# Four reorderings in the mixer of a one-layer hybrid decoder step: state update, decay heads 2 and 3, the copy out of the transposes, and the rank of the convolution's window copies

## The chip, the cores and the metric

The kernel runs on one core of a Trainium2 chip. The metric is the device time of one execution in microseconds (us), as the median of the runs shown. TensorE appears in the profile as PE (matmuls) and PEld (weight loads), VectorE as DVE, ScalarE as ACT, GpSimd as POOL, and the queue of the sync engine, which starts most DMA transfers, as SP.

## What is computed

One layer of a decoder, applied to a prompt of 16 + 256 tokens and to 8 running sequences of 8 new tokens each, 336 token columns in all. The layer projects the normalised input once and feeds two branches, a Conformer convolution and a Mamba-2 mixer, joins them, and then runs a mixture over 16,384 single-row experts (PEER). The change lies in the two branches:

```
c = causal_depthwise(conf_cat, conf_dw_w, conf_dw_b)          # 31 taps, 1024 channels
xbc_c = silu(causal_depthwise(m_cat, m_conv_w, m_conv_b))      # 4 taps, 4096 channels
...
acs   = cumsum(dt * A)                                         # per head
decay = exp(where(causal, acs[t] - acs[s], -inf))
y     = einsum((C B^T) * decay, dt * x) + einsum(C, h) * exp(acs)
h_new = exp(last) * h + einsum(B, w_end * dt * x)              # state update
```

The 32 heads form 8 groups of 4. After the mixer come the two output projections, the join, and the experts: for 128 tokens the chosen expert rows are gathered from HBM, and for the other tokens all experts are computed densely from streamed blocks.

## The kernel before, in words

**Layout.** Channels lie on the 128 partitions and tokens on the free axis. Each of the 80 blocks of 128 output channels of the input projection is one `project()` call: 24 matmuls of 336 (or 320) columns into one PSUM tile of the tag `pj`, which has three buffers. The weights are split in two parts, `wh` (ACT, L243) and `wl` (mostly POOL, L247), with two buffers each, so that a projection multiplies high by high, high by low and low by high.

**The groups.** A loop over the 8 head groups overlaps two things: the projections of the next group and the state-space work of the present one. `ssd(g, ...)` (L617) is a generator whose steps are separated by `yield`; after each projection the loop advances it by one step (`run(new, 1)`), and its last steps run among the next group's projections (`run(old, 1)`). In one group the projections are, in this order: the convolution's value and gate blocks (`conf`, L583), four blocks of x, B and C (`xbc`, L556), and two blocks of the output gate z (`zproj`, L574). The steps of `ssd`, numbered from 0:

- 0: spread the sample tokens of x and B; `decay(0)`, `decay(1)`
- 1: `turn(0)` (three transposes of chunk 0), `decay(2)`
- 2: `turn(1)`, `turn(2)`, `decay(3)`, copies of C
- 3: `running()` (the states of the 8 sequences), `inner(0)`
- 4 and 5: `inner(1)`, `state(0)`; `inner(2)`, `state(1)`
- 6: `state(2)`, `out(0)`
- 7: `out(1)`
- 8: squares of the output, `update()` (eight matmuls and four adds into the states `st`), the DMA of `st` to HBM
- 9: the norm's sum over channels (`pgn`)

**What sets the order.** The PE instructions of the mixer keep the order of the program text. On the other engines a scheduler orders the instructions at build time by priority and by its own estimate of when each is ready; every engine then executes its list strictly in order, and a wait at the head of a list holds up all behind it. `tc.cur_priority` is the rank that the scheduler uses; instructions made while it is raised by `LOW` (400) come later where there is a choice. `act()` (L219) also keeps its activations in program order, and an `ACT_TABLE_LOAD` stands in front of an activation when its function is not in the table that is loaded; exponential and sigmoid or SiLU need different tables.

**PSUM tiles that the steps share.** `pj` has three buffers: every projection takes one and, in `xbc`, keeps it until the SiLU of the short convolution has been read from it, because the convolution's taps are accumulated in the same tile (`conv_short`, L522). `misc` has two buffers (transposes, `pcb`, `pst`, `pq`). `y` has two (`pdec`, `py`, `po`). `update()` takes two `misc` and two `pj` tiles. `pb` has one, for the long convolution.

**The long convolution.** `conv_long` (L504) first copies the 31-column windows of its input into the tile `ch` (`windows`, L494: ACT copies at L499 and L501), then does the first tap on ACT (L517) and the other 30 on DVE (L519), all at low rank. Its result for the last channel block is needed by `norm_mean` (L817) in the last group, in front of the normalisation and of the output projection `conf_out` (L807).

Of the kernel before, what the change touches and what calls it, by code (L numbers as in the profile page):

```python
# [60 lines left out]
LOW = 400  # L61
# [97 lines left out]
def body(tc, ia, oa, stop=None):  # L159
    nc = tc.nc  # L160
    with ExitStack() as top:
# [189 lines left out]
        p = misc([128, T], "pn1")  # L351
# [137 lines left out]
        def samp(ap):  # L489
            return ap.rearrange("p (q c) -> p q c", q=NQ)  # L490
# [3 lines left out]
        def windows(cat):  # L494
            win = mp.tile([128, KD * T2], F32, name="ch")[:, :NCH * WIN]
            wv = win.rearrange("p (c i) -> p c i", i=WIN)
            a_ = cat[:, NM:NM + 1]
            np_ = SQ // TS
            nc.scalar.copy(wv[:, :np_], bass.AP(tensor=a_.tensor, offset=a_.offset,  # L499
                                                ap=[list(a_.ap[0]), [TS, np_], [1, WIN]]))  # L500
            nc.scalar.copy(wv[:, np_:], samp(cat[:, CC + TP:]))  # L501
            return wv

        def conv_long(cat, j, dst):  # L504
            wv = windows(cat)
            acc = ps.tile([128, T], F32, name="pcv", tag="pb", bufs=1)[:, :T2]
            at = tc.cur_priority
            tc.cur_priority = at + LOW

            def eights(v):  # L510
                return v.rearrange("p (c i) -> p c i", i=TS)

            for w in range(CW):
                sc = V("conf_w", j * CW + w)
                in_, to = wv[:, :, w:w + TS], eights(dst if w == CW - 1 else acc)
                if w == 0:
                    nc.scalar.activation(to, in_, AF.Identity, scale=sc, bias=V("conf_b", j))  # L517
                else:
                    nc.vector.scalar_tensor_tensor(to, in_, sc, eights(acc), op0=OP.mult, op1=OP.add)  # L519
            tc.cur_priority = at  # L520
# [96 lines left out]
        def ssd(g, xg, bc, sz):  # L617
# [8 lines left out]
            def decay(r):  # L626
                h = 4 * g + r
                pb = ps.tile([128, T], F32, name="pdec", tag="y", bufs=2)[:, :T2]
                mm(pb, id3[:, h:h + 1].to_broadcast([128, 128]), acs3[:, :T2], start=True, stop=True)
                hs_ = slice(r % 2 * 64, r % 2 * 64 + 64)  # L630
                act(e2[hs_, r // 2], pb[hs_], AF.Exp)
                for i, (t0, L) in enumerate(OTILES):
                    nc.vector.scalar_tensor_tensor(dec[:, r, t0:t0 + L], pb[:, t0:t0 + L], acs[i][:, h:h + 1],
                                                   mneg[:, t0:t0 + L], op0=OP.add, op1=OP.add)
                if r % 2:
                    act(dec[:, r - 1:r + 1], dec[:, r - 1:r + 1], AF.Exp)
# [4 lines left out]
            def turn(i):  # L641
                p = misc([128, 384], "ptr")
                for c_, src in enumerate((xg[:, 0], xg[:, 1], BT)):
                    tr(p[:, c_ * 128:(c_ + 1) * 128], chunk(src, i, c_), ident)
                x_ = sp.tile([128, 384], F32, name=f"xt{i}")
                nc.scalar.copy(x_[:, 256:], p[:, 256:])
                nc.vector.tensor_tensor(r4(x_[:, :256]), r4(p[:, :256]),
                                        dtok[i][:, 4 * g:4 * g + 4, None].to_broadcast([128, 4, P]), op=OP.mult)
                w_ = sp.tile([128, 4, P], F32, name=f"wx{i}")
                nc.gpsimd.tensor_tensor(w_, r4(x_[:, :256]),  # L650
                                        wd[i][:, 4 * g:4 * g + 4, None].to_broadcast([128, 4, P]), op=OP.mult)
                xt.append(x_)
                wx.append(w_.rearrange("p r c -> p (r c)"))
# [29 lines left out]
            def out(b):  # L683
                py = ps.tile([128, T], F32, name="py", tag="y", bufs=2)[:, :T2]
                po = ps.tile([128, T], F32, name="po", tag="y", bufs=2)[:, :T2]
                bs = slice(b * 128, b * 128 + 128)
                for i, (t0, L) in enumerate(OTILES):
                    for r in (2 * b, 2 * b + 1):
                        s = slice((r % 2) * 64, (r % 2) * 64 + 64)
                        mm(py[s, t0:t0 + L], xt[i][:, r * P:(r + 1) * P], dec[:, r, t0:t0 + L],  # L690
                                         start=True, stop=True)
                mm(po[:, SQ:], oq[:, bs], C("selq")[:, :S0], start=True, stop=True)
                for i in (1, 2):
                    t0, L = TILES[i]
                    mm(po[:, t0:t0 + L], hs[i - 1][:, bs], CT[:, t0:t0 + L], start=True, stop=True)
                y = xg[:, b, :T2]
                nc.vector.scalar_tensor_tensor(y, y, V("dskip", 2 * g + b), py, op0=OP.mult, op1=OP.add)
                yo = tp.tile([128, T], F32, name="yo", bufs=2)[:, :T2]
                nc.vector.tensor_tensor(yo, po, e2[:, b], op=OP.mult)
                nc.gpsimd.tensor_tensor(y, y, yo, op=OP.add)  # L700
                nc.gpsimd.tensor_tensor(y, y, sz[:, b, :], op=OP.mult)

            def update():
                four = [f() for _ in range(2) for f in (
                    lambda: misc([128, 512], "pst2"), lambda: ps.tile([128, PJ], F32, name="pst2", tag="pj", bufs=3))]
                for r in range(2):
                    for s_ in range(4):
                        t_ = slice(32 * s_, 32 * s_ + 32)
                        mm(four[s_][:, r * 256:(r + 1) * 256], Bm[t_, r], wx[0][t_], start=True, stop=True)
                for s_ in (1, 3, 0, 2):  # L710
                    sv = st[:, 2 * s_:2 * s_ + 2].rearrange("p q c -> p (q c)")
                    nc.vector.tensor_tensor(sv, sv, four[s_], op=OP.add)  # L712
# [5 lines left out]
            yield  # L718
            turn(0)
            decay(2)  # L720
            yield
            turn(1)
            turn(2)
            decay(3)
            for s_ in range(2):
                nc.scalar.copy(cz[:, 4 * s_:4 * s_ + 4, 8 * s_:8 * s_ + 8],
                               CT[:, SQ + 32 * s_:SQ + 32 * s_ + 32].rearrange("p (q t) -> p q t", q=4))
# [15 lines left out]
            out(0)  # L743
            yield
            out(1)
            yield
            sq = [tp.tile([128, T2], F32, name="sq", bufs=4) for _ in range(2)]
            for b in range(2):
                nc.scalar.activation(sq[b], xg[:, b, :T2], AF.Square)
            nc.gpsimd.tensor_tensor(sq[0], sq[0], sq[1], op=OP.add)  # L750
            update()
            nc.sync.dma_start(oa["ssm_s"][g], st)
            yield
            p = pj2("pgn")
# [178 lines left out]
        for j in range(KD):  # L933
# [4 lines left out]
            p = pj2()  # L938
# [7 lines left out]
        for j in range(KD):  # L946
            w = weight(ia["w_o"], j)
            p = pj2()
# [13 lines left out]
        p = ps.tile([128, T], F32, name="pn2", tag="pb", bufs=1)  # L962
# [38 lines left out]
        for c_ in range(2):  # L1001
            p = misc([128, 512], "px")
# [4 lines left out]
        p = misc([128, 4], "prs")  # L1007
# [178 lines left out]
        for j in range(16):  # L1186
# [5 lines left out]
            p = pj()  # L1192
# [3 lines left out]
            p = misc([128, 3, NK], "psc")  # L1196
# [462 lines left out]
```

## Time and profile before

| what | value |
|---|---|
| runs | 1290.48, 1293.23 and 1297.32 us; median 1293.23 |
| the profiled execution | 1292.4 us; its span, first to last instruction, 1290.6 us |
| busy in the span | PE 1262.9 us, PEld 1217.0, DVE 955.1, ACT 530.0, POOL 602.5 |
| moved by DMA | 373.77 MB, mean 290 GB/s |
| stages, from the chain that ended last | start and first group to about 54 us, groups to 341, last group and output projections to about 540, queries and scores beyond 600, gathers and dense experts to the end |

In the profile a line of a group of instructions gives its program line, engine, operation, the tiles it writes and reads, and the count, then the busy time, the mean of one in ns, and the idle time in front of it with what ended it. In a list of waits a line reads: engine, what waited, what it waited for, the total in us, how many times, the longest. In a timeline a line gives start, duration, engine, line, operation and tiles, and in brackets the idle time in front and what ended it. In the list of stretches a line gives the stretch, its length, the busy time of PE, PEld, DVE, ACT and POOL, the granted clock of TensorE, the share of the DMA engines' time that was busy and the rate in GB/s.

### The profile page before, as it was taken

What the parts mean: (1) busy time and instruction counts of PE and PEld (TensorE: products, weight loads), DVE (VectorE), ACT (ScalarE), POOL (GpSimd) and SP (SyncE); (2) the same over time, 40 slices, a digit from 0 to 9 for tenths busy, and PEclk for the clock granted to TensorE, in tenths of its full rate; (3) what the DMA queues carried; (4) which work ended last, traced back from release to release, by engine and by line L of the source; (5) the groups of instructions that cost most, each with busy time, mean ns of one, the idle gap of its engine ahead of it and who ended that gap; (6) DMA issues with size and microseconds to landing.
All of it is one profiled execution on the core that took longest, in us unless ns stands there. A gap on an engine that the chain in (4) does not pass through costs nothing.

```text
span 1290.6 us, 23645 instructions
## 1 busy us (share of the span) xinstructions
PE 1262.9 (98%) x8951; PEld 1217.0 (94%) x8951; DVE 955.1 (74%) x2095; ACT 530.0 (41%) x1339; POOL 602.5 (47%) x595
## 2 busy tenths in 40 slices
PE   9999999999989999999999998999999999999997
PEld 7999889898879999999999998999999999999996
DVE  6888779877977335549999968878888888545545
ACT  6788877888766444544232211122211111001102
POOL 2487777887784766975132222233333322222220
PEclk9899999999999999999999999999999999999999
DMA  6435444444433444765989999999999999999994
GB/s 250 168 123 190 172 172 160 142 178 168 150 132 134 148 147 149 251 244 208 378 334 416 415 414 416 409 408 410 411 415 416 414 415 414 398 415 414 415 415 158
DMA packets 85905, 373.77 MB, mean 290 GB/s; under 512 B 10000, under 2 KB 15376, under 8 KB 66208
## 3 DMA queue, kind: packets, MB, share of 16 engines
q1 hardware_dynamic: 48336, 166.82, 34.9%
q0 software_dynamic: 19584, 142.62, 27.1%
q10 hardware_dynamic: 17872, 62.84, 12.2%
q8 instruction: 70, 1.15, 0.4%
q14 instruction: 43, 0.35, 0.1%
HBM read 359.18 MB, written 13.06 MB: 288 GB/s over the span
## 4 chain that ended last, share of the span: by engine, by line
PE 60%; DVE 20%; DMA 10%; ACT 6%; issue 3%; POOL 1%; POOLq 0%; ACTq 0%; DVEq 0%; SPq 0%
PE va L1523 23%; PE pj L176 22%; PE pj L1421 11%; DMA wuv<-in_peer_uv_dram,gid 5%; DVE pcv L519 5%; DMA eraw<-in_uT_dram 3%; DVE pj L530 2%; PE pg L1449 2%; DVE wuv L1309 1%; DVE ygat L1319 1%; ACT L219 1%; DMA wuv<-in_fnorm_dram 1%; DVE st L712 1%; ACT wh L243 1%; POOL wl L247 1%
## 5 line engine op out<-in xcount | busy, mean ns | idle before, releaser
L1152 POOL DMA_INDIRECT wuv<-in_peer_uv_dram,gid x136 | 176.7, 1299 | 474.6 <-PE va L1523 107.6
L247 POOL TENSOR_TENSOR wl<-wraw,wh 128x256 fp32r<-128x256 f32 (+1 forms) x202 | 289.1, 1450 | 105.5 <-ACT wh L243 57.4
L1523 PE MATMUL va<-S,eraw 128*128 128x184 f32 x2048 | 325.7, 320 | 1.4 <-DMA eraw<-in_vE_dram 1.4
L1523 PEld LDWEIGHTS va<-S,eraw 128*128 128x128 f32 x2048 | 318.9, 190 | 2.6 <-DMA eraw<-in_vE_dram 1.6
L1421 PE MATMUL pj<-nd,eraw 128*128 128x184 f32 x1792 | 292.1, 322 | 5.5 <-DMA eraw<-in_uT_dram 5.5
L1421 PEld LDWEIGHTS pj<-nd,eraw 128*128 128x128 f32 x1792 | 281.0, 191 | 6.3 <-issue 4.9
L176 PE MATMUL pj<-ah,wh 128*128 128x336 f32 (+1 forms) x768 | 242.4, 326 | 0.5 <-ACT xnf L219 0.3
L176 PE MATMUL pj<-al,wh 128*128 128x336 f32 (+1 forms) x768 | 232.5, 316 | 0.0
L1319 DVE SCALAR_TENSOR_TENSOR ygat<-wuv,scg,ygat 128x1024 f32<-128x1024 f32 x128 | 164.2, 1283 | 68.0 <-ACT scg L1314 66.9
L1311 ACT ACTIVATE scg<-scg 128x1 f32<-128x1 f32 x136 | 27.3, 202 | 426.4 <-DVE wuv L1309 305.6
L1309 DVE SCALAR_TENSOR_TENSOR wuv<-wuv,x2m 128x1024 f32<-128x1024 f32 x128 | 156.3, 1221 | 54.9 <-DMA wuv<-in_peer_uv_dram,gid 52.9
L243 ACT CAST wh<-wraw 128x1024 fp32r<-128x1024 f32 x125 | 131.1, 1050 | 80.1 <-PE pj L176 61.1
L176 PEld LDWEIGHTS pj<-ah,wh 128*128 128x128 f32 x768 | 145.4, 190 | 4.1 <-ACT sz L219 0.7
L176 PEld LDWEIGHTS pj<-al,wh 128*128 128x128 f32 x768 | 145.1, 190 | 0.7
L519 DVE SCALAR_TENSOR_TENSOR pcv<-ch,vec,pcv 128x320 f32<-128x320 f32 x232 | 127.5, 550 | 23.6 <-ACT pcv L517 21.1
L176 PE MATMUL pj<-ah,wl 128*128 128x336 f32 (+1 forms) x768 | 138.0, 315 | 0.0
L176 PEld LDWEIGHTS pj<-ah,wl 128*128 128x128 f32 x768 | 120.5, 189 | 0.3 <-POOL wl L247 0.2
L1423 ACT ACTIVATE S<-pj 128x184 f32<-128x184 f32 x128 | 38.0, 316 | 109.3 <-PE pj L1421 104.5
L530 DVE SCALAR_TENSOR_TENSOR pj<-mcat,vec,pj 128x360 f32<-128x360 f32 x96 | 56.5, 590 | 4.7 <-ACT pj L528 4.4
L1460 DVE SCALAR_TENSOR_TENSOR S<-pg,S 128x232 f32<-128x232 f32 (+1 forms) x92 | 34.6, 418 | 30.9 <-PE pg L1449 30.9
L219 ACT ACT_TABLE_LOAD x38 | 48.8, 1283 | 0.7
L1314 ACT ACTIVATE scg<-scg,ggw 128x1 f32<-128x1 f32 x136 | 39.7, 294 | 6.9 <-PE va L1523 2.8
(388 smaller groups left out, 1699.6 us busy)
## 6 DMA issues: line engine op xcount, KB each, us to landing
wraw<-in_w_in_dram SPq DMA_DIRECT2D x80, 512.0 KB
eraw<-in_vE_dram SPq DMA_DIRECT2D x64, 512.0 KB
eraw<-in_vE_dram ACTq DMA_DIRECT2D x64, 512.0 KB
eraw<-in_uT_dram SPq DMA_DIRECT2D x60, 512.0 KB
eraw<-in_uT_dram ACTq DMA_DIRECT2D x52, 512.0 KB
st<-in_state_dram SPq DMA_DIRECT2D x8, 1024.0 KB
out_ssm_s_dram<-st SPq DMA_DIRECT2D x8, 1024.0 KB
wraw<-in_w_mo_dram SPq DMA_DIRECT2D x16, 512.0 KB
```

The lines of the kernel that those rows point to most:

```text
L176: i_ = nc.tensor.matmul(*a_, **kw)
L219: i_ = nc.scalar.activation(out, in_, f, **kw)
L243: (nc.vector.tensor_copy if on_dve else nc.scalar.copy)(h, src)
L247: (nc.gpsimd if on_pool else nc.vector).tensor_tensor(l[:, q:q + m], src[:, q:q + m], h[:, q:q + m].bitcast(F32), op=OP.subtract)
L519: nc.vector.scalar_tensor_tensor(to, in_, sc, eights(acc), op0=OP.mult, op1=OP.add)
L530: nc.vector.scalar_tensor_tensor(o, cat[:, w:w + n], wv, o, op0=OP.mult, op1=OP.add)
L1152: i_ = nc.gpsimd.indirect_dma_start(out=u, out_offset=None, in_=ia["peer_uv"], in_offset=bass.IndirectOffsetOnAxis(ap=gid[:, c:c + 1], axi ...
L1309: nc.vector.scalar_tensor_tensor(u[:, :D], u[:, :D], 1.0, x2m if c < NPICK else x2e, op0=OP.mult, op1=OP.mult, accum_out=w)
L1314: nc.scalar.activation(w, w, AF.Copy, scale=ggw[:, c:c + 1])
L1319: nc.vector.scalar_tensor_tensor(a_, u[:, D:], scg[:, c:c + 1], a_, op0=OP.mult, op1=OP.add)
L1421: i_ = nc.tensor.matmul(p[:, :ND], raw[:, k, :], nd[:, k, :], start=(k == 0), stop=(k == KD - 1))
L1523: i_ = nc.tensor.matmul(va[k // 2][:, k % 2], raw[:, k, :], Sv(b), start=(b == 0 and k % 2 == 0), stop=(b == 127), skip_group_check=True)
```

## The change

Four edits, all in the mixer. The two copies at the head of `conv_long` get the low rank that its taps already have. The copy of the B part of each transpose, `x_[:, 256:]`, goes from ACT to DVE, so that DVE alone reads the transposed PSUM tile. `decay(3)` moves from step 2 to step 1, next to `decay(2)`. `update()` moves from step 8 to step 7, behind `out(1)`; the DMA of the states stays in step 8.

```
         def conv_long(cat, j, dst):
+            at = tc.cur_priority
+            tc.cur_priority = at + LOW
             wv = windows(cat)
             acc = ps.tile([128, T], F32, name="pcv", tag="pb", bufs=1)[:, :T2]
-            at = tc.cur_priority
-            tc.cur_priority = at + LOW
...
                 x_ = sp.tile([128, 384], F32, name=f"xt{i}")
-                nc.scalar.copy(x_[:, 256:], p[:, 256:])
+                nc.vector.tensor_copy(x_[:, 256:], p[:, 256:])
...
             turn(0)
             decay(2)
+            decay(3)
             yield
             turn(1)
             turn(2)
-            decay(3)
...
             out(1)
+            update()
             yield
...
             nc.gpsimd.tensor_tensor(sq[0], sq[0], sq[1], op=OP.add)
-            update()
             nc.sync.dma_start(oa["ssm_s"][g], st)
```

**ACT, head of a group.** This is ACT's list from the exponentials of the fifth group's first two heads to the sigmoid of the following convolution gate. `e_2774` is the tile of the exponentials `exp(acs)`, `dec` the decay matrices, `xt_...` the transposed chunks, `xnf` the sigmoid. Before:

```order
L219 ACT_TABLE_LOAD
L219 ACTIVATE e_2774<-pdec 64x320 x2
L219 ACTIVATE dec<-dec 128x640
L243 CAST wh<-wraw 128x1024
L646 COPY xt_2830<-ptr 128x128
L219 ACTIVATE e_2774<-pdec 64x320
...
L219 ACT_TABLE_LOAD
L219 ACTIVATE xnf<-pj,vec 128x336
L646 COPY xt_2926<-ptr 128x128
L646 COPY xt_2935<-ptr 128x128
L219 ACT_TABLE_LOAD
L219 ACTIVATE e_2774<-pdec 64x320
```

And in the changed kernel:

```order
L219 ACT_TABLE_LOAD
L219 ACTIVATE e_2774<-pdec 64x320 x2
L243 CAST wh<-wraw 128x1024
L219 ACTIVATE dec<-dec 128x640
L219 ACTIVATE e_2774<-pdec 64x320 x2
L733 ACTIVATE Bm<-xt_2830,cstm 128x128 x3
L243 CAST wh<-wraw 128x1024
L219 ACTIVATE dec<-dec 128x640
L219 ACT_TABLE_LOAD
L219 ACTIVATE xnf<-pj,vec 128x336
```

All four heads' exponentials now stand in front of the sigmoid, the table load behind the sigmoid is gone, and so are the three copies `xt`. Over the whole list ACT has 42 table loads where it had 49.

**PE, end of a group.** This is PE's list from the last matmuls of `out(1)` of the second group to the following `decay(0)`. `pst_...` are the four PSUM tiles of `update()`, each written twice; `pj` between them is the second z block. Before:

```order
L176 MATMUL po<-bc,hs_1538 128x128
L176 MATMUL pj<-ah,wh 128x320
...
L176 MATMUL pj<-ah,wl 128x320 x8
L176 MATMUL pst_1696<-wx_1246,Bm 128x256
L176 MATMUL pst_1697<-wx_1246,Bm 128x256
L176 MATMUL pst_1698<-wx_1246,Bm 128x256
L176 MATMUL pst_1699<-wx_1246,Bm 128x256
...
L176 LDWEIGHTS id_566
```

And in the changed kernel:

```order
L176 MATMUL po<-bc,hs_1538 128x128
L176 MATMUL pst_1658<-wx_1246,Bm 128x256
L176 MATMUL pst_1659<-wx_1246,Bm 128x256
L176 MATMUL pst_1660<-wx_1246,Bm 128x256
L176 MATMUL pst_1661<-wx_1246,Bm 128x256
...
L176 MATMUL pj<-ah,wh 128x320
...
L176 MATMUL pj<-ah,wl 128x320 x8
L176 LDWEIGHTS id_566
```

The eight matmuls of the update have moved in front of one projection of 24 matmuls. The two `pj` tiles that they take are now the ones after the first z block, not after the second.

**POOL and DVE, last group.** Two short pieces of the eighth group, the last. On POOL, `xg` is the gated output (L700 and L701, once for each half), `sq` the sum of its squares that `pgn` on PE reads, `wl` the low parts of weights in quarters. Before and then after:

```order
L247 TENSOR_TENSOR wl<-wraw,wh 128x256 x4
L700 TENSOR_TENSOR xg<-xg,yo 128x320
L247 TENSOR_TENSOR wl<-wraw,wh 128x256 x4
L701 TENSOR_TENSOR xg<-xg,sz 128x320
L750 TENSOR_TENSOR sq<-sq 128x320
```

```order
L247 TENSOR_TENSOR wl<-wraw,wh 128x256 x4
L700 TENSOR_TENSOR xg<-xg,yo 128x320
L701 TENSOR_TENSOR xg<-xg,sz 128x320
L751 TENSOR_TENSOR sq<-sq 128x320
L247 TENSOR_TENSOR wl<-wraw,wh 128x256 x8
```

The sum of squares no longer stands behind four quarters of weights. On DVE, `hs_4687` is the chunk state that the second half of `out(0)` reads, and `ccat<-cbuf,ch` are two splits of the normalised convolution. Before and then after:

```order
L841 TENSOR_TENSOR cbuf<-cbuf,rs 128x320 x5
L670 TENSOR_TENSOR hs_4687<-hs_4687,pst 128x256
L247 TENSOR_TENSOR ccat<-cbuf,ch 128x320 x2
L247 TENSOR_TENSOR sz<-cbuf,ch 128x320
L697 SCALAR_TENSOR_TENSOR xg<-xg,vec,py 128x320
```

```order
L841 TENSOR_TENSOR cbuf<-cbuf,rs 128x320 x5
L247 TENSOR_TENSOR ccat<-cbuf,ch 128x320 x2
L670 TENSOR_TENSOR hs_4687<-hs_4687,pst 128x256
L247 TENSOR_TENSOR sz<-cbuf,ch 128x320
L697 SCALAR_TENSOR_TENSOR xg<-xg,vec,py 128x320
```

The chunk state has moved behind the two splits. On SP the DMA of the states stands one weight load earlier in each group; behind the mixer the lists of all engines are the same but for a few neighbours that change places.

More of the change, by code (lines that the diff above doesn't have):

```diff
@@ L504, in conv_long @@
         def conv_long(cat, j, dst):
+            at = tc.cur_priority
+            tc.cur_priority = at + LOW
             wv = windows(cat)
             acc = ps.tile([128, T], F32, name="pcv", tag="pb", bufs=1)[:, :T2]
-            at = tc.cur_priority
-            tc.cur_priority = at + LOW
             def eights(v):
@@ L645, in turn @@
                 x_ = sp.tile([128, 384], F32, name=f"xt{i}")
-                nc.scalar.copy(x_[:, 256:], p[:, 256:])
+                nc.vector.tensor_copy(x_[:, 256:], p[:, 256:])
                 nc.vector.tensor_tensor(r4(x_[:, :256]), r4(p[:, :256]),
@@ L720, in ssd @@
             decay(2)
+            decay(3)
             yield
@@ L723, in ssd @@
             turn(2)
-            decay(3)
             for s_ in range(2):
@@ L745, in ssd @@
             out(1)
+            update()
             yield
@@ L750, in ssd @@
             nc.gpsimd.tensor_tensor(sq[0], sq[0], sq[1], op=OP.add)
-            update()
             nc.sync.dma_start(oa["ssm_s"][g], st)
```

## The prediction

> **What bounds the kernel now.** I read the page first: the span and the shares of the chain that ended last.
>
> ```profile
> span 1290.6 us, 23645 instructions
> PE 60%; DVE 20%; DMA 10%; ACT 6%; issue 3%; POOL 1%; POOLq 0%; ACTq 0%; DVEq 0%; SPq 0%
> ```
>
> The change lies in the head groups, so I cut that part into stretches from one second z projection to the next, which are six equal rounds of work on TensorE (289 weight loads each).
>
> ```profile
> 89.16:128.22 39.06, 39.06 (x290) 36.27 (x289) 33.26 (x76) 31.44 (x77) 28.88 (x34) 1.00 0.49 173
> 128.22:168.85 40.63, 39.84 (x290) 36.26 (x289) 32.61 (x76) 32.15 (x81) 31.96 (x35) 1.00 0.46 166
> 168.85:208.66 39.81, 39.37 (x291) 36.25 (x289) 32.58 (x74) 32.27 (x80) 30.20 (x33) 1.00 0.46 166
> 208.66:249.54 40.88, 40.10 (x291) 36.27 (x289) 33.88 (x79) 32.29 (x81) 32.17 (x36) 1.00 0.45 162
> 249.54:289.14 39.60, 39.14 (x291) 36.23 (x289) 32.68 (x76) 32.52 (x81) 32.69 (x34) 1.00 0.46 167
> 289.14:329.32 40.18, 39.45 (x290) 36.21 (x289) 33.69 (x77) 31.54 (x78) 29.56 (x32) 1.00 0.49 172
> ```
>
> PE is busy for 39 of some 40 us at a granted clock of 1.00, DVE for 33, ACT for 32. The six rounds sum to 240.16 us. The shortest has no idle PE at all; six like it would take 234.36 us, so all reordering inside these rounds can give about 5.8 us, unless PE itself gets less to do, and it doesn't. What PE waits for by name is in the list of waits, first from 55 to 341 us, then from 341 to 430, the last group and the first output projections.
>
> ```profile
> PE pdec L176 <- DVE dec L633: 3.2, 6, 0.8
> PE pcb L176 <- DVE dec L660: 0.6, 1, 0.6
> PE ptr L181 <- DVE xt L647: 0.2, 1, 0.2
> PE pst L176 <- DVE hs L667: 0.2, 1, 0.2
> ...
> PE pgn L176 <- POOL sq L750: 2.0, 1, 2.0
> PE po L176 <- DVE hs L670: 2.0, 1, 2.0
> PE pj L176 <- DVE cbuf L519: 1.2, 1, 1.2
> PE pj L176 <- POOL wl L247: 0.4, 1, 0.4
> ```
>
> That is 4.2 us and 5.6 us, 9.8 in all: the ceiling of this change by waits that have a name. The Trainium skill (Perfetto Trace Analysis, Identifying the Most-Contended Engine) says that matmul busy time misjudges TensorE's headroom and that weight-load busy time shows it. By that the rounds would have 240.16 - 217.49 = 22.7 us of room, an estimate with the sum of the PEld column; but the shortest round, with the same 36.27 us of weight loads, still has matmuls end to end for 39.06 us, so I go by the waits.
>
> **State update one step earlier.** In step 8 the update's four adds on DVE stand right in front of the next group's decay sums, and `decay(2)` on PE needs the PSUM tile that `decay(0)` fills and those sums empty.
>
> ```profile
> 255.72 0.68 DVE L712 TENSOR_TENSOR st<-st,pst 128x512 f32<-128x512 f32 x1
> 256.77 1.87 DVE L712 TENSOR_TENSOR st<-st,pst 128x512 f32<-128x512 f32 x3
> 259.02 1.24 DVE L633 SCALAR_TENSOR_TENSOR dec<-pdec,acs,mneg 128x64 f32<-128x64 f32 x5
> 259.87 0.31 PE L176 MATMUL pdec<-acs,id 128*128 128x320 bf16 x1 [0.46 <-DVE dec L633]
> ...
> 339.81 0.31 PE L176 MATMUL pdec<-acs,id 128*128 128x320 bf16 x1 [0.77 <-DVE dec L633]
> ```
>
> The matmuls that those sums read are issued at 254.31 (row below); without 2.55 us of adds in front the sums end by about 257, and PE asks at 259.41 (259.87 less its wait). So the 3.2 us go, in five of six cases. The sixth, at 339.81, lies just ahead of `norm_mean`, where PE waits next for the convolution's last tap (`cbuf`, 1.2 us in the list); arriving 0.7 us earlier only lengthens that. I count 3.2 - 0.7 = 2.5 us, between 1.6 (half) and 3.2.
>
> What the move adds is a wait for PSUM. The second and fourth tile of the update are the `pj` tiles of the last two x/B/C blocks, free when their SiLU has read them.
>
> ```profile
> 248.84 0.59 DVE L530 SCALAR_TENSOR_TENSOR pj<-mcat,vec,pj 128x360 f32<-128x360 f32 x1
> 249.12 0.66 PE L176 MATMUL po<-bc,hs 128*128 128x128 f32 x4
> 249.44 0.47 ACT L749 ACTIVATE sq<-xg 128x320 f32<-128x320 f32 x1 [1.29 <-POOL xg L701]
> 249.82 0.55 ACT L219 ACTIVATE bc<-pj 128x256 f32<-128x256 f32 x3
> 250.25 0.54 ACT L219 ACTIVATE sz<-pj,vec 128x320 f32<-128x320 f32 x1
> 253.24 1.15 PE L176 MATMUL pst<-wx,Bm 32*128 32x256 f32 x16
> 254.31 0.45 PE L176 MATMUL pdec<-acs,id 128*128 128x320 bf16 x2
> ```
>
> The last tap ends at 249.43. ACT then reads a square that waits for POOL, and only after it the SiLU `bc`; in the changed list the square stands behind both, so the SiLU would end near 250.0. PE would be through `out(1)` at 249.78 and reach the fourth tile after three of the update's 16 matmuls (1.15 us for all), near 250.0 too: almost even. The stretch of DVE's list from the first to the last tap of the four blocks is one long-convolution tap shorter in most groups, which helps. I take 0.1 us a group, 0.8 in eight. Bounds: 0, and the SiLU ending where `sz` ends now (250.79), 0.8 a group, 6.4. The z projection behind it needs the first z block's SiLU, some 0.4 us after `bc`, while the update's matmuls take 1.15 us: covered. Queued behind the waiting matmul is all of PE.
>
> The squares now stand in front of a weight cast and of the table load on ACT, so the exponentials of heads 0 and 1 come about one cast (1050 ns, below) later than the 256.7 of now.
>
> ```profile
> 253.62 0.47 ACT L749 ACTIVATE sq<-xg 128x320 f32<-128x320 f32 x1 [0.40 <-POOL xg L701]
> 255.81 0.89 ACT L219 ACTIVATE e<-pdec 64x320 f32<-64x320 f32 x2
> L243 ACT CAST wh<-wraw 128x1024 fp32r<-128x1024 f32 x125 | 131.1, 1050 | 80.1 <-PE pj L176 61.1
> 246.17 10.11 SPq L273 DMA_DIRECT2D wraw<-in_w_in_dram  x3
> ```
>
> They let go of the same PSUM tile at 257.8, 1.6 us before `decay(2)` asks: hidden; if the square's wait for POOL grew by 2 us, it would cost 0.4 a group. On SP the DMA of the states now precedes the third weight load. It waits for adds that end one projection earlier than the 258.64 of now, about when the third load is issued (the three end at 256.28); and casts idle for PE (61.1 of 80.1 us), not for weights: nothing.
>
> **Heads 2 and 3 together; copies to DVE.**
>
> ```profile
> L219 ACT ACT_TABLE_LOAD x33 | 42.3, 1283 | 0.6
> L646 ACT COPY xt<-ptr 128x128 f32<-128x128 f32 x24 | 5.5, 267 | 0.2
> L667 DVE COPY hs<-pst 128x256 f32<-128x256 f32 x8 | 3.3, 416 | 0.0
> ```
>
> Seven of the loads go, 7 x 1.283 = 9.0 us of ACT, with 24 copies, 6.4 us. Both lie beside PE work: ACT idles 8 us a round. What they release is `dec`'s exponential, hence the 0.6 us of `pcb`; I count it whole. DVE gains 24 copies at between 0.27 (ACT's) and 0.42 us (DVE's own twice as wide), 6.4 to 10.0 us, 0.8 to 1.25 a group; DVE has 7 us idle a round, so I price them at nothing here and keep the price for the rival. `decay(3)`'s added wait on PE is for `dec(1)`, ended by 257 as above.
>
> **Window copies at low rank.** They are ordered by the scheduler among the short convolutions; with the load gone they still start early. The wait of 1.2 us for the last tap shrinks or not; the lists differ by about one tap there. I take 0.4, between 0 and 1.2.
>
> **Last group.** Two list changes count.
>
> ```profile
> 367.77 0.41 DVE L670 TENSOR_TENSOR hs<-hs,pst 128x256 f32<-128x256 f32 x1
> 368.10 1.50 DVE L247 TENSOR_TENSOR ccat<-cbuf,ch 128x320 fp32r<-128x320 f32 x2
> 379.03 2.83 POOL L247 TENSOR_TENSOR wl<-wraw,wh 128x256 fp32r<-128x256 f32 x4
> 381.83 0.85 POOL L701 TENSOR_TENSOR xg<-xg,sz 128x320 f32<-128x320 f32 x1
> ```
>
> On POOL 2.83 us of weights leave the way of the square sum, more than the 2.0 us that `pgn` waits: 2.0 off, between 1.0 and 2.0. On DVE the chunk state falls behind 1.50 us of splits, and PE waits for it already: 1.5 on, between 0 and 1.5.
>
> **The sum.** -2.5 - 0.6 - 0.4 - 2.0 + 0.8 + 1.5 = -3.2 us. The profiled execution, 1292.4 us (1290.6 of span), becomes 1289.2; the median of the runs shown, 1293.23, becomes 1290.0, my forecast. Nothing after the mixer changes, and it shifts as a whole if it is fed by what comes before.
>
> **Rivals.** A measurement of this kernel can tell about 0.5%, 6.5 us, from no change; so none of this is large.
>
> - *All waits go and none comes* (0.22): -9.8, 1283.4. For it: ACT gets 15.4 us lighter and DVE waits for it now. Against: two lists put something in front of what PE wants.
> - *ACT's time comes back whole* (0.03): -15.4, 1277.8, if PE's unnamed gaps follow ACT. ACT's 32 us in rounds of 40 speak against it. The Trainium skill (ScalarE: Activation LUTs, Table sets: the hidden batching unit) says to batch activations by table set, as this change does; that promises time only where ACT bounds.
> - *Slower by PSUM* (0.12): the update's tiles come late. DVE's copies push the last short-convolution taps back by up to 1.25 us, all eight updates wait on PE, and a projection with them. The gains without the 0.8 are 4.0 us, so it decides at 0.5 us a group; at 1.3 it gives 10.4 - 4.0 = +6.4, 1299.6. For it: the margin worked out above is nil. Against: DVE's idle time lies ahead of the taps, and the square leaves the SiLU's way.
> - *Hidden anyway* (0.11): the experts' DMA sets its own end; 1293.2. For it, the stretch where gathers and blocks are fetched:
>
> ```profile
> 672.00:803.00 131.00, 125.38 (x868) 123.41 (x866) 111.08 (x253) 30.14 (x111) 34.19 (x29) 0.99 1.02 414
> ```
>
> The DMA engines are full there. Against: the gathers need indices that come out of the mixer, so a full queue starts earlier too.
>
> **Numbers.** The forecast has 0.52, its own range 1287 to 1293. The range 1284 to 1297 holds it, the hidden case, more than half of the first rival and the mild half of the slower one, about 8 in 10. Faster by over 0.5% is most of the first two rivals and a tail of the forecast, 0.25; slower is the stronger part of the third, 0.10; the rest, 0.65, is within.
>
> **What would show it.** Right: PE's wait for `dec` L633 under 1 us in all, `pgn` without a wait, `po` for `hs` L670 at 3 to 4 us, rounds of about 39.5, seven table loads fewer, the second half shifted by the same amount. Wrong: a wait of PE's `pst` or of the z projection for ACT of over 0.5 us a group, rounds at or over 40, or an end that doesn't follow the mixer's.

## The result and the profile after

The changed kernel takes 1287.72 us (median of 5 runs, 1286.42 to 1289.07) against 1293.23: a ratio of 0.9947, 95% interval 0.9931 to 0.9963. Measured again later it gave 0.9958 (0.9941 to 0.9975). The profiled execution took 1286.42 us.

The page's span and the shares of the chain that ended last, after:

```profile
span 1284.7 us, 23645 instructions
...
PE 76%; DVE 11%; DMA 8%; issue 2%; POOL 1%; ACT 1%; ACTq 0%; POOLq 0%; SPq 0%; DVEq 0%
```

The span is 5.9 us shorter. ACT's share of the chain fell from 6% to 1% and DVE's from 20% to 11%. The same six rounds as before, from one second z projection to the next (columns: PE, PEld, DVE, ACT, POOL busy; clock; DMA share; GB/s):

```profile
91.58:130.56 38.98, 38.98 (x292) 36.33 (x288) 34.21 (x80) 30.78 (x76) 29.86 (x34) 1.00 0.49 173
130.56:170.50 39.94, 39.34 (x291) 36.30 (x287) 34.54 (x81) 30.82 (x76) 32.21 (x35) 1.00 0.46 169
170.50:209.48 38.98, 38.98 (x292) 36.34 (x288) 33.56 (x78) 31.09 (x76) 30.91 (x32) 1.00 0.48 169
209.48:249.36 39.88, 39.25 (x291) 36.20 (x287) 34.53 (x81) 30.73 (x76) 32.39 (x37) 1.00 0.46 166
249.36:288.32 38.96, 38.96 (x291) 36.32 (x287) 33.90 (x80) 30.71 (x75) 32.18 (x34) 1.00 0.48 170
288.32:327.97 39.65, 39.13 (x292) 36.23 (x288) 34.48 (x80) 30.42 (x73) 30.73 (x33) 1.00 0.49 178
sum 236.39, PE 234.64 PEld 217.71 DVE 205.22 ACT 184.55 POOL 188.27; mean PE 39.11 PEld 36.29 DVE 34.20 ACT 30.76 POOL 31.38
```

They fell from 240.16 to 236.39 us, and they alternate: three have no idle PE at all (38.97), three are 0.7 to 1 us longer. PE's waits, from 55 to 341 us and then from 341 to 430:

```profile
PE pdec L176 <- DVE dec L633: 3.3, 9, 0.5
PE pj L176 <- ACT xg L219: 1.2, 1, 1.2
...
PE pj L176 <- POOL wl L247: 2.3, 5, 0.7
```

The wait that the largest term of the prediction removed, `pdec` for `dec`, is as long as before (3.3 us against 3.2). What went are `pcb`, `ptr`, `pst`, `pgn`, `po` and the wait for `cbuf`; a new one came, for the SiLU `xg` in the first round, and the wait for `wl` in the last group grew from 0.4 to 2.3 us.

A round is counted here from 1, a group in the code (`j`, `g`) from 0. For all kernels below I read three marks off PE's timeline: the first `pdec` of the first group, that of the last group, and the last matmul `pgb` (the broadcast of the group norm, behind the eight gates). Before, the seven rounds between the first two take 279.91 us and the last group to the third 81.49; after, 277.55 (-2.4) and 78.41 (-3.1), together -5.4 of the span's -5.9. Behind the mixer the whole program shifts. These marks come from one profile of each kernel; the last section says what the clock of TensorE can add to one of them.

### The profile page after: what moved, and what is told of

Its sections match the earlier page's. It is cut to its first block, busy times and chain, and to the rows that moved or that the text cites. A ratio compares the mean times of both kernels' runs of the same rounds, so it can differ in the third digit from the quotient of the medians.

```text
span 1284.7 us, 23645 instructions
## 1 busy us (share of the span) xinstructions
PE 1260.9 (98%) x8951; PEld 1217.3 (95%) x8951; DVE 961.1 (75%) x2119; ACT 520.3 (40%) x1308; POOL 600.3 (47%) x595
## 3 DMA queue, kind: packets, MB, share of 16 engines
q8 instruction: 70, 1.15, 0.4%
## 4 chain that ended last, share of the span: by engine, by line
PE 76%; DVE 11%; DMA 8%; issue 2%; POOL 1%; ACT 1%; ACTq 0%; POOLq 0%; SPq 0%; DVEq 0%
PE pj L176 32%; PE va L1523 23%; PE pj L1421 13%; DMA wuv<-in_peer_uv_dram,gid 4%; DMA eraw<-in_uT_dram 3%; DVE ygat L1319 2%; PE pg L1449 2%; DVE wuv L1309 1%; DVE pcv L519 1%; PE pst L176 1%; DMA eraw<-in_vE_dram 1%; PE po L176 1%; PE py L176 1%; PE pq L176 1%; DMA wdt<-in_w_dt_dram 1%
## 5 line engine op out<-in xcount | busy, mean ns | idle before, releaser
L1152 POOL DMA_INDIRECT wuv<-in_peer_uv_dram,gid x136 | 170.6, 1254 | 481.8 <-PE va L1523 121.7
L1421 PE MATMUL pj<-nd,pre 128*128 128x184 f32 x256 | 42.0, 319 | 0.0
```

The costliest lines, as they stand in the source:

```text
L1152: i_ = nc.gpsimd.indirect_dma_start(out=u, out_offset=None, in_=ia["peer_uv"], in_offset=bass.IndirectOffsetOnAxis(ap=gid[:, c:c + 1], axi ...
L1421: i_ = nc.tensor.matmul(p[:, :ND], raw[:, k, :], nd[:, k, :], start=(k == 0), stop=(k == KD - 1))
```

## The experiments

The number that opens each result is the ratio of its time to that of the kernel before, run beside it on the same chip, with a 95% interval. The first four: each of three edits alone, and the changed kernel with the disputed convolution taps moved.

**1. The update's move alone.**

```
             out(1)
+            update()
             yield
...
-            update()
             nc.sync.dma_start(oa["ssm_s"][g], st)
```

> The kernel before with the state update's move alone. Theory A (each engine runs its list; what stands ahead decides): DVE's list here has 4 or 7 convolution taps where the four state adds stood ahead of the decay sums, so PE's wait for dec stays in the rounds with 7 taps, about 3 us in all against 3.2 before; the seven rounds to the start of the last group change by no more than 0.7 us in sum. In the last group POOL's square sum stands ahead of the weight parts, as in the changed kernel: pgn without a wait, and a wait for wl of about 2 us in a later projection; net -1.5 to -3 us. In all -1 to -3.5 us. Theory B (the adds were the whole cause, as predicted): PE's wait for dec falls under 1 us in all and the rounds give 2 to 3 us more, -3.5 to -6 in all.

0.9983 (0.9971 to 0.9994); rounds 280.32, last group 78.37. The wait for `dec` stays (2.8 us) and the last group is 3.1 us shorter, by theory A. Not expected by either theory: the wait for PSUM that the prediction's slower rival named is here. ACT and PE at the end of the second group:

```profile
126.57 0.47 ACT L750 ACTIVATE sq<-xg 128x320 f32<-128x320 f32 x1 [1.26 <-POOL xg L701]
126.87 1.80 PE L176 MATMUL pst<-wx,Bm 32*128 32x256 f32 x16
126.94 0.55 ACT L219 ACTIVATE bc<-pj 128x256 f32<-128x256 f32 x3
127.55 0.72 PEld L176 LDWEIGHTS pst<-wx,Bm 32*128 32x128 f32 x10 [0.37 <-ACT bc L219]
```

ACT stands 1.26 us at the square, which waits for POOL; the SiLU `bc` behind it ends at 127.49, and the update's matmuls, 1.15 us long where nothing waits, take 1.80. In six of eight groups they are 0.3 to 0.9 us longer, 3.8 us in all. So the rounds stay within the 0.7 us of theory A (+0.4) only because two things cancel: this wait, and some 4 us that went elsewhere, 2.2 of them between the second and the fourth x/B/C projection. That the adds' move is worth nothing in the rounds is not shown.

**2. `decay(3)` alone.**

```
             decay(2)
+            decay(3)
             yield
             turn(1)
             turn(2)
-            decay(3)
```

> The kernel before with decay(3) moved beside decay(2) alone: 42 table loads on ACT where there were 49. Theory A: the exponentials of heads 2 and 3 come early, so the small gaps of PE from the second x projection to the first z projection go, which the traces of before and after put at about 4.4 us over seven rounds: the last group starts 2.5 to 4.5 us earlier than before; the last group itself is as before (pgn still waits 2 us). Theory B (that gain needs the copies off ACT as well): the last group starts less than 1.5 us earlier.

1.0014 (1.0000 to 1.0028); rounds 280.28, last group 83.04.

```profile
PE pdec L176 <- DVE dec L633: 5.3, 11, 0.9
```

Half of theory A holds: from the second round to the seventh the stretches from the second to the fourth x/B/C projection sum to 51.7 us, as in the changed kernel (51.9), where before has 55.5; these 3.7 us go with `decay(3)` alone. (The update alone takes 2.2 of the same 3.7, run 1, so the two can't be added.) But the last group doesn't start earlier, because the same edit lengthened the wait for `dec` from 3.2 to 5.3 us and brought one of 1.2 us of `pq` for `xt`. `decay(2)` needs the tile of `decay(0)`, `decay(3)` that of `decay(1)`, whose sums end 0.7 to 1.2 us later. In each of the seven rounds of before, of the changed kernel and of runs 1, 2 and 5 the gate projection begins either when PE has done its own work (4.7 us behind the value projection, 4.85 with `decay(3)` between them) or 0.1 us behind the end of the sums: those of `decay(0)` where `decay(3)` is not moved, of `decay(1)` where it is. The seven table loads fewer (9.0 us of ACT) bought no time in sum here; no run takes loads out without moving the exponentials. The Trainium skill (ScalarE: Activation LUTs, What ACT_TABLE_LOAD costs) gives about 1283 ns for a load itself, and a drain of about 1380 ns for each switch of table. The trace agrees on the load (1283 ns) and shows no such drain: between 55 and 385 us of before, ACT idles 0.6 us in all in front of 33 loads, and 0.01 us behind each but one. The loads are paid beside PE's work.

**3. The copies alone.**

```
-                nc.scalar.copy(x_[:, 256:], p[:, 256:])
+                nc.vector.tensor_copy(x_[:, 256:], p[:, 256:])
```

> The kernel before with the transposes' copies on DVE alone, 49 table loads as before. Theory A: copies and their releases are covered; the last group starts within 0.7 us of before and PE's waits in the rounds are as before. Theory B (ACT's relief by itself makes the gain): the last group starts 1.5 to 4 us earlier. Theory C (DVE's copies push the sums back): it starts 1 to 3 us later, with PE's wait for dec or xt grown by as much.

1.0036 (1.0022 to 1.0050): slower; rounds 284.31, last group 84.21. The sign is C's, but the last group starts 4.4 us later, more than C said, and C's wait for `xt` grew by 0.9 us only (0.2 to 1.1), while that for `dec` fell. PE's first two waits, and ACT's list ahead of the longest:

```profile
PE pj L176 <- ACT xg L219: 3.0, 2, 1.8
PE pst L176 <- ACT gs L679: 2.2, 3, 1.0
```

```profile
116.92 1.03 ACT L243 CAST wh<-wraw 128x1024 fp32r<-128x1024 f32 x1
117.96 1.28 ACT L219 ACT_TABLE_LOAD   x1
119.26 0.57 ACT L219 ACTIVATE xg<-pj 128x256 f32<-128x256 f32 x3
```

A weight cast and a table load have come to stand in front of the SiLU that frees the tile of the next projection. Before has as many loads; here they only stand elsewhere. Part of the loss is the clock: behind that wait it is 0.50 for 3.4 us (from 121.2 us), and the stretch of the next projection takes 7.27 us instead of 5.75. The changed kernel has the same three rows in its first round:

```profile
76.51 1.06 ACT L243 CAST wh<-wraw 128x1024 fp32r<-128x1024 f32 x1 [1.53 <-issue]
77.59 1.28 ACT L219 ACT_TABLE_LOAD   x1
78.88 0.57 ACT L219 ACTIVATE xg<-pj 128x256 f32<-128x256 f32 x3
```

That is its wait of 1.2 us for `xg`: the projection begins 1.5 us later than in the other rounds.

**4. The taps held back.** The changed kernel, in which the last seven taps of a long convolution are ordered behind the sums of `decay(1)` on the same engine (an ordering in the list, no wait).

```
+        HOLD = 7
...
+            if j in (1, 2, 3, 4, 5, 6):
+                taps(0, CW - HOLD)
+                held.append(lambda d: taps(CW - HOLD, CW, d))
...
             decay(0)
-            decay(1)
+            d = decay(1)
+            for f in held:
+                f(d)
```

> The changed kernel, with the last seven taps of each long convolution but the first and the last ordered behind the decay sums of the next group's heads 0 and 1, on the same engine and with the same work. DVE's list then has 1 to 4 taps ahead of those sums where the changed kernel has 4 or 7. Theory A (the taps took the freed place): PE's wait for dec falls from 3.3 us to about 1 (the last group's round still has its 7 taps), the stretch from the value to the gate projection is 4.8 to 4.9 us in all rounds but the first and the last, and the time falls by 2 to 3 us against the changed kernel. Theory B (decay(2) waits for something else, such as the decay matmuls' own place in PE's list or the exponentials on ACT): the wait stays within 0.7 us of 3.3 and the time within 1 us of the changed kernel's.

0.9983 (0.9971 to 0.9994), slower than the changed kernel by both of its ratios (0.9947 and 0.9958, though the second interval just touches); rounds 276.30, last group 83.13. The mechanism is theory A's (the wait for `dec` falls to 1.7 us), the total isn't. DVE in the third round, first of the changed kernel, then of this one, both from the last add of the update:

```profile
133.35 1.28 DVE L712 TENSOR_TENSOR st<-st,pst 128x512 f32<-128x512 f32 x2
134.54 4.10 DVE L519 SCALAR_TENSOR_TENSOR pcv<-ch,vec,pcv 128x320 f32<-128x320 f32 x7
138.55 1.50 DVE L633 SCALAR_TENSOR_TENSOR dec<-pdec,acs,mneg 128x64 f32<-128x64 f32 x6
```

```profile
132.85 0.68 DVE L731 TENSOR_TENSOR st<-st,pst 128x512 f32<-128x512 f32 x1
133.45 2.33 DVE L525 SCALAR_TENSOR_TENSOR pcv<-ch,vec,pcv 128x320 f32<-128x320 f32 x4
135.68 1.51 DVE L651 SCALAR_TENSOR_TENSOR dec<-pdec,acs,mneg 128x64 f32<-128x64 f32 x6
```

Seven taps (4.10 us) or four (2.33) stand ahead of the sums, though PE's matmuls for them are issued at 134.18 in the changed kernel; with four the sums are in time, and the third and the fifth round (groups 2 and 4) fall from 39.95 and 39.89 us to 38.97 and 38.91. What was lost is elsewhere, in PE's waits of this kernel (55 to 341 us, then 341 to 430):

```profile
PE pj L176 <- ACT xg L219: 2.4, 2, 1.2
PE pj L176 <- DVE cbuf L525: 2.2, 1, 2.2
...
PE po L176 <- DVE hs L689: 3.4, 1, 3.4
```

The taps of the convolution `j` = 6, held back into the seventh round, delay the last convolution (`j` = 7), for whose last tap the last group waits again, and a table load stands in front of an `xg` a second time, in that round; run 8, which doesn't hold these taps, has neither wait.

**5 to 7. The changed kernel without one edit each** (the diffs of 3, 2 and 1 undone in it: `nc.scalar.copy` again; `decay(3)` in step 2 again; `update()` in step 8 again).

> The changed kernel without the move of the transposes' copies (they stay on ACT); 42 table loads. The seven rounds of the changed kernel sum to 277.55 us in its profile, before to 279.92. Theory A (the gain is that of decay and update together, the copies are covered work): the seven rounds sum to 277.0 to 278.5 us, and the sixteen matmuls of the update take 0.77 us in all groups. Theory B (the update's PSUM tiles come in time only because ACT lost the copies): the update's matmuls take 1.2 to 1.7 us in most groups, as in the kernel with the update's move alone (1.08 to 1.67 in six of eight), and the rounds sum to 280 to 282 us.

0.9990 (0.9977 to 1.0003); rounds 279.09, last group 80.09. Between the theories: the update's matmuls take no longer in six of eight groups (0.1 and 0.6 us in two), so B is wrong, but PE's wait for `dec` is 5.5 us, with seven or eight taps ahead of the sums of `decay(1)` in three rounds.

> The changed kernel without the move of decay(3); 49 table loads as before. Theory A (the gaps between the x projections went with decay(3)): they come back, 0.2 to 1.2 us in most rounds, and a table load stands in front of the SiLU that frees a projection's tile in some rounds, as with the copies' move alone: the seven rounds sum to 281 to 285 us against 277.55. Theory B (ACT's relief by the copies is enough): the rounds sum to less than 279 us.

0.9991 (0.9978 to 1.0004); rounds 282.03, last group 78.26: theory A, with gaps back and `pj` waiting 2.7 us for `xg`.

> The changed kernel without the move of the update. Theory A (DVE's list has the adds and one or two taps ahead of the sums in every group, and decay(3) needs them too): PE's wait for dec is 4.5 to 6 us over the rounds, as in the kernel with decay alone (5.3), and the rounds sum to 279.5 to 282 us; in the last group pgn waits 0.5 to 2 us for POOL again. In all 1291 to 1296 us. Theory B (in the rounds the update's move brings nothing, since taps took the freed place): the rounds sum to 277 to 278.5 us and only the last group is 2 to 3 us longer.

1.0014 (0.9998 to 1.0029); rounds 279.14, last group 84.44. The rounds lie between the theories, the wait for `dec` (2.9 us) is less than A said and `xg` costs 2.4; the last group is 6.0 us longer than with the update moved, more than either said (some 1.4 us of it by the clock, which drops once more here than in the changed kernel), with four waits by name:

```profile
PE pj L176 <- DVE cbuf L519: 2.2, 1, 2.2
PE pgn L176 <- POOL sq L750: 2.0, 1, 2.0
PE po L176 <- DVE hs L670: 2.0, 1, 2.0
PE pj L176 <- POOL wl L247: 0.4, 1, 0.4
```

**8. Two places mended.** Taps held back only for the third and the fifth round, the two with seven of them ahead of both sums, and the SiLU's table loaded behind the sigmoid in the first round.

```
+        HOLD = 7
...
+            if j in (2, 4):
+                taps(0, CW - HOLD)
+                held.append(lambda d: taps(CW - HOLD, CW, d))
...
                 act(sg, pb, AF.Sigmoid, bias=V("b_in", 8 * j + 5))
+                if j in (1,):
+                    chain(nc.scalar.preload_act_table_set("silu_and_others"))
```

> The changed kernel with two places mended: the last seven taps of the long convolutions of groups 2 and 4 but the last tap's store ordered behind the decay sums (4 taps ahead where there were 7), and the SiLU's table loaded right behind the sigmoid in the first round; as many loads and taps as in the changed kernel, and the lists otherwise the same. Theory A (what stands ahead in a list decides, also for the load): the rounds of groups 2 and 4 fall from 39.95 and 39.89 us to 38.95, the stretch from the third to the fourth x/B/C projection of the first round from 5.91 to 4.4, the last group as in the changed kernel, the seven rounds to 274.1 us, 3.4 us less; time 1283.5 to 1285. Theory B (the load and the taps fill idle time and something else ends the waits): the first round stays at 41.1 us or its loss moves to the next projection, and the time is within 1.5 us of the changed kernel's.

0.9924 (0.9900 to 0.9948), 1284.9 us: with run 10 the shortest time of all, below both kernels (the changed one has 0.9947 and 0.9958; the intervals still overlap). The seven rounds are 274.18 us, 274.1 expected. Three rounds, those of groups 2 to 4, and the only wait listed for PE from 55 to 341 us:

```profile
127.96:166.94 38.98, 38.98 (x292) 36.33 (x288) 34.26 (x81) 30.72 (x76) 32.27 (x35) 1.00 0.48 173
166.94:205.91 38.97, 38.97 (x291) 36.33 (x287) 33.56 (x78) 31.08 (x76) 30.87 (x32) 1.00 0.48 169
205.91:244.82 38.91, 38.91 (x292) 36.26 (x288) 34.27 (x81) 30.71 (x76) 32.38 (x37) 1.00 0.46 170
```

```profile
PE pdec L176 <- DVE dec L653: 2.1, 5, 0.5
```

The wait for `xg` is gone with the same number of loads: the load now stands where ACT has time, and the first round takes 39.72 us instead of 41.16. The last group takes 79.80 us instead of 78.41, by the clock (below).

**9. The window copies at low rank alone.**

```
+            at = tc.cur_priority
+            tc.cur_priority = at + LOW
             wv = windows(cat)
             acc = ps.tile([128, T], F32, name="pcv", tag="pb", bufs=1)[:, :T2]
-            at = tc.cur_priority
-            tc.cur_priority = at + LOW
```

> The kernel before with the window copies at low rank alone. DVE's list in the rounds is that of before, and so are the table loads. Theory A (this edit carries nothing by itself): the seven rounds within 0.7 us of 279.9, the last group within 1 us of before, the time within 0.15%. Theory B (the copies' old rank was a cost of its own): the rounds 1 to 3 us shorter.

0.9998 (0.9984 to 1.0012); rounds 280.02, last group 81.43. Nothing, by theory A.

**10 and 11. One weight of the last group to DVE**, on top of 8; gate weight 70 in run 10, 71 in run 11.

```
-            on_dve = int((nw[0] + 1) * f_) > int(nw[0] * f_)
+            on_dve = int((nw[0] + 1) * f_) > int(nw[0] * f_) or nw[0] in (70,)
```

> The kernel with the two mended places, and in the last group the low part of one gate weight on DVE, where it costs one instruction of about 1.22 us, in place of four quarters on POOL (3.3 us); it is the weight ahead of the state decays on POOL. DVE's list also puts the chunk state hs ahead of the second normalisation there. Theory A (POOL's list is what the last group's wl waits come from): the five wl waits, 2.3 us, go, and the dip of the granted clock behind them (0.5 to 0.7 for some 4 us) with them; the last group's stretch to its last group-norm broadcast falls from 78.4 (changed kernel) and 79.8 us (two places) to 75 to 77; time 1280 to 1283. Theory B (DVE's normalisation is next in line): the wait goes over to po for hs or to the first output projection, and the stretch stays at 78 to 80 us.

0.9927 (0.9907 to 0.9948), as run 8; last group 81.05: theory B in kind, though the wait went to another place than it named and the stretch is longer than its 80.

```profile
PE py L176 <- DVE xg L718: 3.1, 1, 3.1
PE pj L176 <- ACT xnf L826: 1.6, 1, 1.6
PE pj L176 <- POOL wl L247: 0.4, 1, 0.4
```

PE's wait for POOL fell to 0.4 us, and DVE's eight normalisations in one piece took its place. The edit is not quite the one expected: the low part that DVE makes here (at 348.53) is the one that PE waited for, which POOL made behind the state decays in run 8 (at 354.46). The one ahead of the decays is still POOL's.

> As the kernel before this one, but it is the next weight, the one that the five wl waits are for, that goes to DVE, in front of the second normalisation. Theory A: the five wl waits go, but hs stands as late on DVE as before plus one instruction, so po waits for hs by 1 to 3 us in their place; the stretch is 77.5 to 80 us. Theory B (POOL alone mattered): no new wait, 75 to 77 us.

0.9936 (0.9916 to 0.9957), last group 80.03. Both theories fail: the wait for `wl` grew to 3.0 us. The trace shows why: the edit moved the weight after the one that PE waits for. That one stays on POOL behind the state decays, which take 6.59 us here against 5.87 in run 8, so it comes 0.7 us later; why the decays are longer is open.

**12. The changed kernel again.**

> The changed kernel again, beside the others on the same chip: 1285 to 1290 us by both theories, the seven rounds 277.5 us; a second profile for the clock in the last group (0.5 to 0.9 of full speed for a few us behind the wl waits if that is what lowers it, 1.00 if it was chance).

0.9958 (0.9941 to 0.9975). The first group began 2.6 us earlier and its round took 44.16 us instead of 41.16; the other six are 236.43 against 236.39, so the seven sum to 280.59, not to 277.5. So a start this early is given back in the first round. Both come with the clock: here it is 1.00 from 40 to 54 us, where the changed kernel's first profile has 0.50 for 6.8 us (from 42.7), and it is 0.50 for 3.4 us in the first round (from 58.6), behind a wait of 2.1 us for the sums. The other kernels start between 52.6 and 54.7 us, and there it does little: runs 8 and 10, 1.4 us apart, have first rounds of 39.72 and 39.69 us.

**What follows from the set.** The edits don't add. Against before, rounds and last group together, update alone is -2.7 us, `decay(3)` +1.9, copies +7.1, rank +0.1; the four sum to +6.4, and together they are -5.4. Taken out of the four, the update costs 7.6, `decay(3)` 4.3, the copies 3.2; the rank was not taken out. These are single profiles with different clocks (from the first round to the last `pgb` run 3 has 13.7 us at half clock, before and the changed kernel have 3.4 each, run 1 has none), so the sizes are rough. The ratios, from five to ten runs of each kernel, say the same: -0.17, +0.14, +0.36 and -0.02% sum to +0.31%, and together they are -0.53 and -0.42%.

## Why the prediction was right, and where it was not

The time was right (1290.0 forecast, 1287.7 measured, within the range) and so was the rounds' sum: -2.5 - 0.6 + 0.8 = -2.3 forecast, -2.4 measured. The terms under it were not: the rounds' sum came out by luck, since the wait that was to go stayed and a gain priced at 0.6 us was six times as large. The gain in all, 5.5 us by the medians against 3.2 forecast, was undersized in the last group.

**State adds out of the way (-2.5): wrong.** The step that failed is "without 2.55 us of adds in front the sums end by about 257". The adds did leave. The scheduler filled the place with 4 to 7 convolution taps (2.3 to 4.1 us), presumably since by its own estimate DVE was free there; no run shows that estimate. Runs 4 and 8 show what the taps do: with fewer taps the wait goes. The price of that is 0.95 us in the third and the fifth round each and some 0.7 in the seventh.

**`decay(3)`'s added wait, "ended by 257 as above": wrong for the same reason.** Run 2 shows that it moves PE's point of waiting from the sums of `decay(0)` to those of `decay(1)`, from 3.2 to 5.3 us with the adds in place.

**The exponentials earlier (-0.6): right in kind, six times too small.** I priced the named wait `pcb`; run 2 gives 3.7 us from the second round on. Most of it stood where the list of waits has no name (a projection after another in 4.64 or 4.98 us instead of 4.28): in gaps that are too short for it, and in matmuls that start later one behind the other, which the profile counts as busy. PE's busy time in the six rounds of before is 236.95 us, where six of the shortest would have 234.36.

**PSUM wait of the update (+0.8): right in size, 0.1 us a group, but by another cause** (the two z stretches together 9.95 instead of 9.86). No update waits for PSUM in the changed kernel: its matmuls take 1.15 us in every group, as before. The 0.1 us lies where PE changes from one kind of matmul to another (0.17 more in front of the update, 0.09 less behind the z projection, in the fifth round). And "in the changed list the square stands behind both" is true for two of seven groups only; in the others the square stands ahead and doesn't wait, because the output it squares is ready. The rival's mechanism is real: run 1 shows it at 0.3 to 0.9 us in six groups, about the 0.5 at which I let it decide. With either the copies' or `decay(3)`'s move beside it most of it is gone (runs 6 and 5: 0.5 and 0.7 us in all).

**Table loads and copies (0): right for the sum of the time, wrong for its place.** Run 2 has seven loads fewer and is no faster, and a DVE copy costs 0.28 us in the changed kernel, inside the bounds:

```profile
L646 DVE COPY xt<-ptr 128x128 f32<-128x128 f32 x24 | 6.7, 280 | 1.2 <-PE ptr L181 1.2
```

But a load in another place makes PE wait 1.2 us (changed kernel) or, with a cast, 1.8 us (run 3), and moving it alone gave 1.4 us back (first round of run 8). No term held that.

**Last group (-0.4 - 2.0 + 1.5 = -0.9): -3.1 measured.** The named waits from 341 to 430 us fall from 5.6 to 2.3 us. The wait for `cbuf` went whole, 1.2 us, and `pgn` lost its 2.0, as forecast. The wait of `po` for `hs` didn't grow by 1.5 but went, 2.0 us: PE came later, held by `wl`, 1.9 us more than before, which no term held. POOL's eight state decays (5.86 us) stand in front of that weight. The clock drops to 0.50 for 3.4 us once in each kernel, behind `pgn` before and behind `wl` after, so it hardly enters the difference. The gain goes with the update's move: without it the last group takes 81.4 to 84.4 us (before and runs 2, 3, 7 and 9), with it 78.3 to 80.1 (the changed kernel and runs 1, 5, 6, 8 and 12); run 4, with 83.13, pays for the taps it holds back.

**Rivals.** "All waits go" is out: 3.3 us remain. "ACT's time comes back whole" is out by run 2. "Hidden anyway" is out: the second half shifted. Of the signs I named, `pgn`, the loads, the shift and rounds of about 39.5 us (39.4 in the mean) came true; the wait for `dec` under 1 us, `po` at 3 to 4 us didn't.

## What to carry to other kernels

When an instruction is moved out of another's way and a scheduler makes the lists, read what the new list puts into the place before you count the wait as gone; DVE's list in the changed kernel has the taps there. Price work on an engine off the critical path by its place, not its length: a kernel with 9 us fewer of table loads was no faster (run 2), while one load in front of an instruction that frees a PSUM tile cost 1.4 (run 8). And measure edits together and one by one where they share engines: here the copies' move was a loss alone (1.0036), `decay(3)` no gain (1.0014, 1.0000 to 1.0028), and taking either out of the four loses time.

## What the hardware showed

The granted clock of TensorE falls to half behind some waits. Two stretches of before, each with 2.0 us of waits in it, and what follows, cut where the clock changes:

```profile
366.00:368.30 2.30, 0.28 (x3) 0.09 (x2) 2.30 (x4) 2.30 (x5) 2.30 (x3) 1.00 0.15 61
368.30:372.00 3.70, 3.70 (x26) 3.68 (x26) 3.70 (x7) 3.67 (x7) 3.70 (x6) 1.00 0.44 146
...
382.00:384.30 2.30, 0.26 (x2) 0.13 (x2) 0.65 (x2) 1.57 (x3) 1.54 (x2) 1.00 0.65 150
384.30:387.70 3.40, 3.40 (x11) 3.01 (x12) 1.92 (x3) 1.59 (x2) 0.00 (x0) 0.50 0.97 384
387.70:390.00 2.30, 2.30 (x17) 2.30 (x17) 0.00 (x0) 1.02 (x1) 0.00 (x0) 0.99 0.52 201
```

Behind the first wait the clock stays at 1.00, behind the second it is 0.50 for 3.4 us. From the start of `pgn` to that of the second projection behind it PE takes 5.74 us there; at 1.00, in the changed kernel, it takes 4.07. The waits for `wl` do the same, in the changed kernel and in run 8, whose last group has the same lists and is equal to it within 0.01 us up to these waits:

```profile
360.00:363.50 3.50, 2.30 (x10) 1.48 (x10) 3.50 (x5) 2.74 (x6) 3.50 (x4) 1.00 0.00 0
363.50:366.90 3.40, 3.40 (x21) 2.51 (x20) 3.40 (x6) 3.38 (x7) 3.40 (x5) 0.50 0.48 159
366.90:370.00 3.10, 3.10 (x23) 3.10 (x23) 2.76 (x6) 3.09 (x7) 3.10 (x5) 1.00 0.49 166
```

```profile
354.80:358.20 3.40, 1.68 (x6) 0.89 (x6) 3.40 (x6) 2.79 (x7) 3.40 (x4) 0.99 0.00 0
358.20:365.00 6.80, 6.63 (x31) 5.65 (x32) 6.54 (x11) 6.63 (x12) 6.80 (x9) 0.50 0.39 127
```

The slow stretch lasts 3.4 us in the changed kernel and 6.8 in run 8, which is 1.39 us longer from here on. In run 12, the changed kernel again, it lasts 6.8 us too (from 362.4). So the drop goes with these waits in all three, and its length changes from run to run. From the first round to the last `pgb`, every such stretch of the fourteen profiles follows 1.2 to 2.4 us of idle PE within the 3.4 us in front of it. The reverse doesn't hold: run 5 has a wait of 2.7 us (at 365.4) and a clock of 1.00 behind it. The Trainium skill (TensorE: Matmul & The Clock Gate, What's actually happening) describes a clock halved after an idle window of about 3.4 us whose phase is not tied to the program: the half agrees, and so do stretches of 3.4 us and twice that, but here 2.0 us of idle PE were enough once and not the other time. So a wait of PE of 2 us can cost 3.7, and two profiles of one kernel can differ by 1 us here (the last group of the changed kernel takes 78.41 us in its first profile and 79.45 in run 12).
